# The rotary embedding of the latent keys: from the head of the query part to the place behind its projection

## The chip, the cores and the metric

The kernel runs on one core of a Trainium2 chip. The metric is the device time of one execution in microseconds (us), as the median of several runs. Engines are named as the profile names them: PE (TensorE, matrix products; PEld are its weight loads), DVE (VectorE), ACT (ScalarE), POOL (GpSimd) and SP (which only issues transfers). Each engine works through its own instructions in a fixed order, and an instruction that has to wait for another engine holds up everything behind it on its own engine.

## What is computed

One layer of a decoder with 512 positions and width 1024: a norm and an input projection, three causal token mixers side by side (RWKV-7, "FoX" forgetting attention with 4 heads of 64, and multi-head latent attention, MLA, with 4 heads), a gated merge, an output projection and a squared-ReLU MLP. The part that the change touches is the rotary embedding of the MLA keys. Cut to that:

```
q_lat, kv_lat, k_pe = split(z_c, [384, 384 + 256])        # k_pe: 64 columns, shared by all heads
q  = (rms_norm(q_lat) @ w_q_up).reshape(B, S, 4, 128 + 64)
q_pe = apply_rope(q[..., 128:], cos, sin)
k_pe = apply_rope(k_pe, cos, sin)
apply_rope(x) = concat([x1 * cos - x2 * sin, x1 * sin + x2 * cos])   # x1, x2: halves of the last axis
```

`k_pe` has 64 numbers for each of the 512 positions. The rotated keys are needed when the MLA logits are formed, the rotated queries likewise.

## The kernel before

All products are made of three matmuls each (`mm3`, lines 146 to 150): operands are split into a high and a low float32r part, and high x high, low x high and high x low are added up. ACT makes the high part and DVE the low part (`hilo`, L120 and L121), both for the weights that arrive by DMA (`wraw` to `whi` and `wlo`) and for intermediate results.

The 512 positions are 4 tiles of 128 (`NT = 4`). The order around the change is this:

1. `attn_inputs` (from L479). A product with the columns `wn` gives, for each tile of positions, 324 columns in PSUM: FoX values, the 64 columns of `k_pe` and the 4 forget gates. L521 copies the key columns to `kpe`, in four ACT instructions, one for each tile. Then `log_forget` computes the forget gates; in it POOL clears the tile `lfx` (L614), DVE copies the gates into it (L616), and PE makes their running sum from it (L627, `pcum`).
2. `attention` (from L644). A loop over heads and tiles issues logits, softmax, transposes and the product with the values, a few steps apart. Between them `fill` hands PE pieces of other projections ("fillers"): first the remaining RWKV columns, then the second pair of FoX heads (`fox_steps`), then `mla_prep`.
3. `mla_prep` (L767) is the head of the query part of MLA. It first issues the rotary embedding of the keys, for one tile of positions after the other: two products with cosine and sine (L777, L778) into a scratch tile `rope`, and a difference and a sum (L779, L780) into `kr`, all on POOL. Then, for each tile, PE makes the 256 rotary query columns in an accumulator `acc`, DVE multiplies them with cosine and sine (L777 and L778 again, with DVE as the engine), and POOL takes difference and sum into `qr`. At the end PE transposes `kr` (L799).

PE's order is written out by hand (`manual_schedule`). DVE, ACT, POOL and SP follow an order that a scheduler derives from the program; it is fixed when the kernel is built.

The scratch tile `rope` is one of the tiles `wk` (L483): 128 x 512 numbers, five buffers, used in turn also for the probabilities `p` of the softmax (L705), for `lfx`, `cum` and others. A new tile takes a buffer when the last reader of its former content is done; for a `p` this is its transposition on PE (L717, `tp<-ident,p`). The transposes have a single buffer in PSUM (`tp`): the next one waits until ACT (L721, `pth`) and DVE (L722, `ptl`) have read the one before.

Of the kernel before, what the change touches and what calls it, by code (L numbers as in the profile page):

```python
# [12 lines left out]
F32 = mybir.dt.float32  # L13
# [5 lines left out]
ALU = mybir.AluOpType  # L19
# [4 lines left out]
P = 128  # L24
S = 512
NT = S // P
# [72 lines left out]
class Builder:  # L99
# [379 lines left out]
    def attn_inputs(self, pz, zps):  # L479
        nc, a, ap = self.nc, self.a, self.ap  # L480
        self.omu = self.cp.tile([P, 16], F32, name="omu")[:, 0:8]
        nc.vector.tensor_scalar(self.omu, self.col("mu", 0, 8), -1.0, 1.0, ALU.mult, ALU.add)
        wk = lambda name: ap.tile([P, S], F32, tag="wk", name=name, bufs=5)  # L483
        self.wk = wk
        self.cstep = wk("cstep")
        nc.sync.dma_start(self.cstep, a["cstep"])
        h = self.h
        self.vt = lambda name: ap.tile([P, S], F32R, tag="v", name=name, bufs=8)
        self.fv = [self.vt(f"fv{t}") for t in range(NT)]
        wn = self.stream(a["wn"], NCG, into=[(self.vt("nh"), self.vt("nl")) for i in range(2)])  # L490
        wns = [next(wn) for i in range(WN_AHEAD)]
        lraw = [ap.tile([P, 3, S], F32, tag="pth", name="lraw", bufs=2) for _ in range(2)]
        lat = [lraw[i // 3][:, i % 3] for i in range(5)]
        for i in range(5):
            if i in LAT_DVE:
                nc.vector.tensor_copy(lat[i], zps[i])
            else:
                nc.scalar.activation(lat[i], zps[i], AF.Copy)
        self.qk = lambda name: ap.tile([P, S], F32R, tag="qk", name=name, bufs=12)
        self.fqk = [None] * 4  # L500
        self.fox_queries(0, zps[5])
        self.fox_keys(0, zps[6])
        self.kpe = ap.tile([P, NT, 64], F32, name="kpe")
        self.lf = ap.tile([P, NT, 8], F32, name="lf")[:, :, 0:4]
        pn = [pz.tile([P, NCG], F32, tag="z", name=f"n{t}") for t in range(NT)]
        self.lat = [None] * 5
        norms = [self.lat_norm(pz, lat, at, n, g) for at, n, g in ((0, 3, "qg"), (3, 2, "kvg"))]
        for kb in range(NB):
            whi, wlo = wns.pop(0)
            for t in range(NT):  # L510
                sl = slice(t * P, (t + 1) * P)
                self.mm3(pn[t], (h[0][kb][:, sl], h[1][kb][:, sl]), (whi, wlo), kb == 0, kb == NB - 1)
            wns += [w for w in (next(wn, None),) if w]
            self.some_mods(MODS_N if kb < MODS_K else 0)
            if kb in (1, 2):
                next(norms[kb - 1])
            if kb in (5, 6):
                next(norms[kb - 5])
        for t in range(NT):
            nc.vector.tensor_tensor(self.lf[:, t, :], pn[t][:, 320:324], self.col("bf", 0, 4), ALU.add)  # L520
            nc.scalar.activation(self.kpe[:, t, :], pn[t][:, 256:320], AF.Copy)  # L521
        for t in range(NT):
            fv = self.fv[t].rearrange("p (h q f) -> p h q f", h=4, q=2)
            self.hilo(fv[:, :, 0], fv[:, :, 1], pn[t][:, 0:256].rearrange("p (h f) -> p h f", h=4))
        self.log_forget()
        self.ksq = []
        self.feed = self.pieces([(a["wz"][:, (2 + i) * D:(3 + i) * D], D) for i in range(2)] + self.attn_weights())
        self.ahead = None
        self.weight()
        for i in range(2):  # L530
            ps = pz.tile([P, S], F32, tag="z", name="zz")
            for kb, _ in enumerate(self.z_steps(i, ps)):
                if (i, kb) == NORM_AT:
                    for norm in norms:
                        for _ in norm:
                            pass
                if (i, kb) == CUM_AT:
                    self.forget_cumsum(pz)

    def fox_queries(self, pair, ps):  # L540
        nc = self.nc
        for hh in range(2):
            own, oth = slice(hh * 64, hh * 64 + 64), slice(64 - hh * 64, 128 - hh * 64)
            qa, qb, ka, kb = self.fqk[2 * pair + hh] = [self.qk(n) for n in ("fqa", "fqb", "fka", "fkb")]
            nc.scalar.activation(qa[own], ps[own], AF.Copy, scale=0.125)
            nc.vector.scalar_tensor_tensor(qa[oth], ps[own], 0.125, qa[own].bitcast(F32), ALU.mult, ALU.subtract)
            nc.scalar.activation(qb[own], ps[own], AF.Copy, scale=0.125)
# [219 lines left out]
    def mla_prep(self):  # L767
        nc, a, ap, wk = self.nc, self.a, self.ap, self.wk

        def rope(src, t, nh, dst, eng):  # L770
            c = self.cos[:, t, None, None, :].broadcast_to([P, nh, 2, 32])
            s = self.sin[:, t, None, None, :].broadcast_to([P, nh, 2, 32])
            tt = wk("rope").rearrange("p (x h two f) -> p x h two f", x=2, h=4, two=2)
            t1, t2 = tt[:, 0, 0:nh], tt[:, 1, 0:nh]
            v = src.rearrange("p (h two f) -> p h two f", h=nh, two=2)
            d = dst.rearrange("p (h two f) -> p h two f", h=nh, two=2)
            eng.tensor_tensor(t1, v, c, ALU.mult)  # L777
            eng.tensor_tensor(t2, v, s, ALU.mult)  # L778
            nc.gpsimd.tensor_tensor(d[:, :, 0], t1[:, :, 0], t2[:, :, 1], ALU.subtract)  # L779
            nc.gpsimd.tensor_tensor(d[:, :, 1], t2[:, :, 0], t1[:, :, 1], ALU.add)  # L780

        self.lath = ([x[0] for x in self.lat], [x[1] for x in self.lat])
        kr = ap.tile([P, NT, 64], F32, name="kr")
        for t in range(NT):
            rope(self.kpe[:, t, :], t, 1, kr[:, t], nc.gpsimd)
        wqr = self.weight()
        self.qr = qr = ap.tile([P, NT, 256], F32, name="qr")
        for t in range(NT):
            tl = slice(t * P, (t + 1) * P)
            ps = self.acct()  # L790
            for kb in range(3):
                wl = slice(kb * 256, kb * 256 + 256)
                self.mm3(ps[:, 0:256], (self.lat[kb][0][:, tl], self.lat[kb][1][:, tl]),
                         (wqr[0][:, wl], wqr[1][:, wl]), kb == 0, kb == 2)
            rope(ps[:, 0:256], t, 4, qr[:, t], nc.vector)
            yield 1.5 * MM3
        pk = self.prw.tile([P, S], F32, tag="rw", name="pk")
        for t in range(NT):
            nc.tensor.transpose(pk[0:64, t * P:(t + 1) * P], kr[:, t], self.ident)  # L799
        self.k1 = k1 = ap.tile([P, S], F32R, name="k1")  # L800
        nc.scalar.activation(k1[0:64], pk[0:64], AF.Copy)
        nc.vector.tensor_tensor(k1[64:128], pk[0:64], k1[0:64].bitcast(F32), ALU.subtract)
# [843 lines left out]
```

## Time and profile before

| | |
|---|---|
| three runs | 876.29, 876.34, 876.96 us (median 876.34) |
| the profiled execution | 875.69 us, of which 873.9 us are the span from the first instruction to the last |
| PE busy | 845.9 us, 97% of the span |
| DVE, ACT, POOL busy | 524.8, 381.5, 95.6 us |
| mean granted PE clock | 0.989 of full speed |

A row of the timeline gives the start in us, the duration, the engine, the line, the operation, output and input tiles, shapes and the count. In brackets stands how long the engine had stood idle before the row, and what ended that. A row of a table by stage gives the stretch and its length, for each engine its busy time with the number of instructions, the granted PE clock, the share of the DMA engines and the GB/s. PE's matmuls overlap each other: the distance from start to start is the cost of one, not its duration.

### The profile page before, as it was taken

How to read it: one execution, taken by the hardware profiler on the slowest of the kernel's cores; microseconds unless marked ns; L12 is line 12 of the kernel's file. 1: busy time of each engine (PE TensorE's matmuls, PEld its weight loads, DVE VectorE, ACT ScalarE, POOL GpSimd, SP SyncE). 2: the span in 40 equal slices, each digit the busy share in tenths (PEclk: the TensorE clock that was granted, in tenths of full speed). 3: DMA queues.
4: the chain of work that ended last, by engine and by line, in shares of the span. 5: the costliest groups of instructions: out<-in, count | busy, mean ns of one | idle time of the engine just before them, and what ended most of it. 6: DMA issues, size and time to landing. Idle time of an engine off the chain costs nothing.

```text
span 873.9 us, 12074 instructions
## 1 busy us (share of the span) xinstructions
PE 845.9 (97%) x4520; PEld 699.8 (80%) x4520; DVE 524.8 (60%) x1053; ACT 381.5 (44%) x855; POOL 95.6 (11%) x129
## 2 busy tenths in 40 slices
PE   8889996999999999999999999999999999999997
PEld 6668786788877888886788889888888888888886
DVE  6998865887489755344586686442236543233465
ACT  5458663765462232424654775432314343122331
POOL 4410003000021089200000110000000000000000
PEclk9999997999999999999999999999999999999999
DMA  9764221111246732311136402432246432333311
GB/s 353 244 216 168 66 64 40 42 62 52 96 134 210 258 111 91 115 50 49 32 109 223 169 25 77 141 97 84 88 145 214 144 121 85 97 106 98 97 49 72
DMA packets 32635, 102.56 MB, mean 117 GB/s; under 512 B 5873, under 2 KB 7553, under 8 KB 31810
## 3 DMA queue, kind: packets, MB, share of 16 engines
q1 hardware_dynamic: 32002, 100.94, 34.9%
q0 software_dynamic: 288, 0.79, 0.3%
q8 instruction: 35, 0.57, 0.3%
q14 instruction: 22, 0.18, 0.1%
q10 hardware_dynamic: 288, 0.08, 0.0%
HBM read 99.16 MB, written 2.63 MB: 116 GB/s over the span
## 4 chain that ended last, share of the span: by engine, by line
PE 84%; DVE 9%; ACT 3%; issue 2%; DMA 1%; POOL 1%; SPq 0%; DVEq 0%; POOLq 0%; ACTq 0%
PE acc L148 24%; PE acc L150 23%; PE acc L149 23%; DVE wm L219 2%; DVE wlo L463 1%; PE z L472 1%; PE tp L717 1%; DMA xt<-xT 1%; DVE hl L464 1%; DVE mod L428 1%; PE pu L1027 1%; PE pr L1186 1%; DMA wm<-wmod 0%; PE py L1203 0%; PE pv L734 0%
## 5 line engine op out<-in xcount | busy, mean ns | idle before, releaser
L121 DVE TENSOR_TENSOR wlo<-wraw,whi 128x512 fp32r<-128x512 f32 (+4 forms) x260 | 165.6, 656 | 197.5 <-ACT whi L120 197.1
L120 ACT ACTIVATE whi<-wraw 128x512 fp32r<-128x512 f32 (+4 forms) x260 | 145.3, 587 | 295.1 <-PE acc L149 178.1
L148 PE MATMUL acc<-g,whi 128*128 128x512 f32 (+1 forms) x304 | 108.3, 356 | 0.0
L149 PE MATMUL acc<-g,whi 128*128 128x512 f32 (+1 forms) x304 | 108.1, 356 | 0.0
L150 PE MATMUL acc<-g,wlo 128*128 128x512 f32 (+1 forms) x304 | 108.1, 356 | 0.0
L148 PE MATMUL acc<-hh,whi 128*128 128x512 f32 x256 | 105.2, 411 | 0.0
L150 PE MATMUL acc<-hh,wlo 128*128 128x512 f32 x256 | 100.4, 392 | 0.6 <-DVE wlo L121 0.6
L149 PE MATMUL acc<-wlo,uh 128*128 128x512 f32 (+1 forms) x262 | 100.8, 385 | 0.0
L148 PE MATMUL acc<-whi,uh 128*128 128x512 f32 (+1 forms) x262 | 100.7, 384 | 0.0
L150 PE MATMUL acc<-whi,ul 128*128 128x512 f32 (+1 forms) x262 | 100.7, 384 | 0.0
L149 PE MATMUL acc<-hl,whi 128*128 128x512 f32 x256 | 100.1, 391 | 0.0
L219 DVE SCALAR_TENSOR_TENSOR wm<-wm,crow 128x1024 f32<-128x1024 f32 x41 | 52.2, 1274 | 24.1 <-DMA wm<-wmod 24.1
L148 PEld LDWEIGHTS acc<-g,whi 128*128 128x128 f32 x304 | 57.5, 189 | 8.2
L150 PEld LDWEIGHTS acc<-g,wlo 128*128 128x128 f32 x304 | 57.5, 189 | 8.1
L149 PEld LDWEIGHTS acc<-g,whi 128*128 128x128 f32 x304 | 57.5, 189 | 8.1
L150 PEld LDWEIGHTS acc<-hh,wlo 128*128 128x128 f32 x256 | 48.1, 188 | 11.7 <-DVE wlo L121 1.0
L149 PEld LDWEIGHTS acc<-wlo,uh 128*128 128x128 f32 x262 | 49.2, 188 | 10.1 <-DVE wlo L121 0.4
L150 PEld LDWEIGHTS acc<-whi,ul 128*128 128x128 f32 x262 | 49.2, 188 | 9.8
L148 PEld LDWEIGHTS acc<-whi,uh 128*128 128x128 f32 x262 | 49.2, 188 | 9.8
L148 PEld LDWEIGHTS acc<-hh,whi 128*128 128x128 f32 x256 | 48.5, 190 | 10.1 <-issue 0.2
L149 PEld LDWEIGHTS acc<-hl,whi 128*128 128x128 f32 x256 | 48.3, 189 | 8.1
L706 ACT ACTIVATE p<-sc,nb 128x128 f32<-128x128 f32 (+3 forms) x32 | 16.8, 526 | 28.3 <-DVE nb L704 14.7
(435 smaller groups left out, 1485.9 us busy)
## 6 DMA issues: line engine op xcount, KB each, us to landing
wm<-wmod SPq DMA_DIRECT2D x36, 512.0 KB, 4.3
wraw<-wu SPq DMA_DIRECT2D x32, 512.0 KB, 3.3
wraw<-wd SPq DMA_DIRECT2D x24, 512.0 KB, 3.3
wraw<-wgb SPq DMA_DIRECT2D x16, 512.0 KB, 3.4
wm<-wmod SPq DMA_DIRECT2D x6, 1024.0 KB, 6.8
wraw<-wz SPq DMA_DIRECT2D x10, 512.0 KB, 3.4
wraw<-wga SPq DMA_DIRECT2D x8, 512.0 KB, 3.6
wraw<-wo SPq DMA_DIRECT2D x8, 512.0 KB, 4.4
```

Of the source, the lines that this page charges most:

```text
L120: nc.scalar.activation(hi, src, AF.Copy)
L121: nc.vector.tensor_tensor(lo, src, hi.bitcast(F32), ALU.subtract)
L148: mm(out, lhs[0], rhs[0], start=start, stop=False)
L149: mm(out, lhs[0], rhs[1], start=False, stop=False)
L150: mm(out, lhs[1], rhs[0], start=False, stop=stop)
L219: self.nc.vector.scalar_tensor_tensor(w, w, 0.5, self.crow[:, cols], ALU.mult, ALU.mult, accum_out=dst)
L428: nc.vector.scalar_tensor_tensor(A, acc[0], b1[:, d:d + 1], self.col("gpre", d), ALU.add, ALU.mult)
L463: nc.vector.tensor_tensor(wlo, raw, whi.bitcast(F32), ALU.subtract)
L464: nc.vector.scalar_tensor_tensor(lo, t, B, hi.bitcast(F32), ALU.add, ALU.subtract)
L472: nc.tensor.matmul(zps[i], w[:, i * P:(i + 1) * P], r, start=first and w is whi and r is hi, stop=last and r is lo)
L706: nc.scalar.activation(p[:, 0:n], ps[:, 0:n], AF.Exp, bias=nb, scale=scale, accum_out=den)
L717: nc.tensor.transpose(tp[:, kb, :], p[:, kb * P:(kb + 1) * P], self.ident)
```

## The change

The key part leaves `mla_prep` and becomes a method of its own, `key_rope`. It is called in `attn_inputs` right behind the four copies into `kpe`. It does all four tiles of positions at once: four POOL instructions (two products over 4 x 64 numbers for each partition, a difference and a sum over 4 x 32), where there were sixteen. It takes one scratch tile `rope`, where the old code took four. The local function `rope` in `mla_prep` is left with the queries alone, and always multiplies on DVE.

```
             nc.scalar.activation(self.kpe[:, t, :], pn[t][:, 256:320], AF.Copy)
+        self.key_rope()
         for t in range(NT):
...
+    def key_rope(self):
+        pool, shp = self.nc.gpsimd, [P, NT, 2, 32]
+        self.kr = self.ap.tile([P, NT, 64], F32, name="kr")
+        tt = self.wk("rope").rearrange("p (x t two f) -> p x t two f", x=2, t=NT, two=2)
+        v, d = (x.rearrange("p t (two f) -> p t two f", two=2) for x in (self.kpe, self.kr))
+        pool.tensor_tensor(tt[:, 0], v, self.cos[:, :, None, :].broadcast_to(shp), ALU.mult)
+        pool.tensor_tensor(tt[:, 1], v, self.sin[:, :, None, :].broadcast_to(shp), ALU.mult)
+        pool.tensor_tensor(d[:, :, 0], tt[:, 0, :, 0], tt[:, 1, :, 1], ALU.subtract)
+        pool.tensor_tensor(d[:, :, 1], tt[:, 1, :, 0], tt[:, 0, :, 1], ALU.add)
...
-            eng.tensor_tensor(t1, v, c, ALU.mult)
-            eng.tensor_tensor(t2, v, s, ALU.mult)
+            nc.vector.tensor_tensor(t1, v, c, ALU.mult)
+            nc.vector.tensor_tensor(t2, v, s, ALU.mult)
...
-        kr = ap.tile([P, NT, 64], F32, name="kr")
-        for t in range(NT):
-            rope(self.kpe[:, t, :], t, 1, kr[:, t], nc.gpsimd)
+        kr = self.kr
...
-            rope(ps[:, 0:256], t, 4, qr[:, t], nc.vector)
+            rope(ps[:, 0:256], t, 4, qr[:, t])
```

On PE, DVE, ACT and SP every instruction keeps its place. Only POOL's order changes. The first excerpt is POOL before, from the last product of the conditioning (`wm`) to the first tile of positions of the key part; three more groups like it follow, and then the query part (`qr`).

```order
L222 TENSOR_TENSOR wm<-wm,crow 128x1024
L614 MEMSET lfx 128x512
L777 TENSOR_TENSOR rope<-kpe,cos 128x64
L778 TENSOR_TENSOR rope<-kpe,sin 128x64
L779 TENSOR_TENSOR kr<-rope 128x32
L780 TENSOR_TENSOR kr<-rope 128x32
```

The second is POOL of the changed kernel at the same place (its lines are shifted: L546 to L549 are `key_rope`, L625 clears `lfx`).

```order
L222 TENSOR_TENSOR wm<-wm,crow 128x1024
L546 TENSOR_TENSOR rope<-kpe,cos 128x256
L547 TENSOR_TENSOR rope<-kpe,sin 128x256
L625 MEMSET lfx 128x512
L548 TENSOR_TENSOR kr<-rope 128x4x32
L549 TENSOR_TENSOR kr<-rope 128x4x32
L790 TENSOR_TENSOR qr<-rope 128x4x32
L791 TENSOR_TENSOR qr<-rope 128x4x32
```

The key part now runs as soon as `kpe` is there, and its two products stand ahead of the clearing of `lfx`.

The third excerpt is DVE of the changed kernel, where `mla_prep` begins: `fkb` belongs to the last FoX head, `rope` is the first tile of the rotary queries, `ptl` the low part of transposed probabilities, `nb` a softmax maximum. These rows stand in the same order before, under the lines 121, 561, 777, 555, 778, 722 and 702.

```order
L121 TENSOR_TENSOR wlo<-wraw,whi 128x512
L572 TENSOR_SCALAR fkb<-cum,cols 64x512
L788 TENSOR_TENSOR rope<-acc,cos 128x256
L566 TENSOR_TENSOR fkb<-acc,fka 64x512
L789 TENSOR_TENSOR rope<-acc,sin 128x256
L733 TENSOR_TENSOR ptl<-tp,pth 128x2x128
L713 TENSOR_REDUCE nb<-sc 128x1
```

Nothing moved here. What differs is what the first `rope` row waits for. Before, its scratch buffer is the one that the last tile of the key part used, so it waits for POOL's last `kr` row and for PE. In the changed kernel the buffer is free of POOL's work: it waits for PE alone, for the two transposes that read the old content.

More of the change, by code (lines that the diff above doesn't have):

```diff
@@ L768, in mla_prep, with rope @@
         nc, a, ap, wk = self.nc, self.a, self.ap, self.wk
-        def rope(src, t, nh, dst, eng):
+        def rope(src, t, nh, dst):
             c = self.cos[:, t, None, None, :].broadcast_to([P, nh, 2, 32])
```

## The prediction

> **What bounds the kernel now.** I read the page first, then PE's waits, then the stretch in which PE stands still, engine by engine.
>
> ```profile
> PE   845.9 (97%) x4520; PEld 699.8 (80%) x4520; DVE 524.8 (60%) x1053; ACT 381.5 (44%) x855; POOL 95.6 (11%) x129
> ...
> PEclk9999997999999999999999999999999999999999
> ```
>
> PE is the bound: 97% of the span. What can be won is either work of PE, which the change leaves alone, or one of its few gaps. One slice of the clock line is not 9: the seventh, from 131 to 153 us, the stretch of the key part. PE's waits by cause, and then its timeline there:
>
> ```profile
> PE z L472 <- ACT hh L462: 7.7, 5, 3.0
> PE tp L717 <- DVE ptl L722: 7.1, 2, 6.9
> ```
> ```profile
> 128.49 0.28 PE L148 MATMUL acc<-whi,lath 128*128 128x256 f32 x1
> ...
> 129.57 0.38 PE L717 MATMUL tp<-ident,p 128*128 128x128 f32 x2
> ...
> 131.31 0.28 PE L150 MATMUL acc<-whi,latl 128*128 128x256 f32 x1
> 138.50 0.87 PE L717 MATMUL tp<-ident,p 128*128 128x128 f32 x3 [6.91 <-DVE ptl L722]
> ...
> 139.71 0.52 PE L148 MATMUL acc<-whi,lath 128*128 128x256 f32 x1
> ...
> 143.65 0.81 PE L717 MATMUL tp<-ident,p 128*128 128x128 f32 x4
> 144.22 0.36 PE L759 MATMUL sc<-fka,fqa 128*128 128x256 f32 x1
> ```
>
> The longest gap of the kernel is here: PE stands still from 131.59 to 138.50, 6.91 us, because the transposes want the one `tp` buffer, which DVE's `ptl` row has not read yet. Who holds up DVE:
>
> ```profile
> 132.09 0.53 DVE L561 TENSOR_SCALAR fkb<-cum,cols 64x512 fp32r<-64x512 f32 x1
> 136.41 0.42 DVE L777 TENSOR_TENSOR rope<-acc,cos 128x256 f32<-128x256 f32 x1 [3.79 <-POOL kr L780]
> 136.87 0.69 DVE L555 TENSOR_TENSOR fkb<-acc,fka 64x512 fp32r<-64x512 f32 x1
> 137.60 0.42 DVE L778 TENSOR_TENSOR rope<-acc,sin 128x256 f32<-128x256 f32 x1
> 137.94 0.41 DVE L722 TENSOR_TENSOR ptl<-tp,pth 128x256 fp32r<-128x256 f32 x1
> ...
> 141.14 0.48 DVE L708 TENSOR_SCALAR p<-p,rden 128x512 f32<-128x512 f32 x1
> ```
> ```profile
> 130.08 0.62 POOL L777 TENSOR_TENSOR rope<-kpe,cos 128x64 f32<-128x64 f32 x1 [55.11 <-PE tp L717]
> ...
> 135.25 0.32 POOL L777 TENSOR_TENSOR rope<-kpe,cos 128x64 f32<-128x64 f32 x1
> ...
> 136.13 0.25 POOL L780 TENSOR_TENSOR kr<-rope 128x32 f32<-128x32 f32 x1
> ```
>
> DVE's rotary query row waits 3.79 us for POOL's last key row, and `ptl` stands three rows behind it. POOL had been idle for 55 us: it could not start because its scratch buffer was held by probabilities until the transposes at 129.57. So the chain is PE's transposes, sixteen POOL rows (130.08 to 136.38), DVE's `rope`, `fkb`, `rope`, `ptl`, PE. The part of the 6.91 us that POOL causes is DVE's 3.79; the other 3.1 is DVE's own queue.
>
> The second cost of the gap is the clock. By stage, with two stretches of the start-up for comparison:
>
> ```profile
> 24.63:28.04 3.41, 0.45 (x3) 0.07 (x1) 3.38 (x4) 0.84 (x2) 1.67 (x1) 1.00 0.83 295
> 28.04:31.45 3.41, 3.41 (x8) 2.71 (x9) 3.34 (x7) 2.46 (x5) 1.05 (x1) 0.50 0.64 178
> 130.43:133.84 3.41, 1.16 (x10) 0.95 (x9) 2.17 (x5) 1.72 (x4) 3.18 (x8) 1.00 0.20 28
> 133.84:137.25 3.41, 0.00 (x0) 0.00 (x0) 0.80 (x2) 0.00 (x0) 2.23 (x9) 0.50 0.17 68
> 137.25:140.67 3.42, 2.17 (x11) 2.20 (x12) 2.49 (x7) 1.76 (x4) 1.70 (x4) 0.50 0.00 0
> 140.67:144.08 3.41, 3.41 (x18) 3.41 (x18) 1.97 (x7) 0.65 (x3) 0.91 (x3) 0.50 0.02 5
> 144.08:147.50 3.42, 3.42 (x23) 3.08 (x23) 2.93 (x8) 2.29 (x6) 0.88 (x2) 1.00 0.00 0
> ```
>
> The granted clock (the column behind POOL's) is 1.00 or 0.50 over whole stretches of 3.41 us, and all its changes lie on one grid of that step: down at 28.04, up at 31.45, down at 133.84, up at 144.08 (133.84 is 31 steps behind 28.04). A stretch in which PE works 0.45 or 1.16 us is followed by half clock. One with 3.41 us of work is followed by full clock, one with 2.17 us (at half clock) is not. So after the gap PE runs at half clock from 138.50 to 144.08.
>
> **The change part by part.**
>
> *The sixteen POOL rows go from the gap.* DVE's `rope` row then waits for PE alone, for transposes that started at 129.57, and for its accumulator, done by then. DVE reaches the row when the `fkb` row ends, 132.09 + 0.53 = 132.62, instead of 136.41. Nothing between it and `ptl` waits for anything new (the high part of `fkb`, which ACT makes, comes nearest; its row is the first below), so `ptl` and PE's restart move from 138.50 to about 134.73. **Term 1: 3.77 us.** A gap of 131.59 to 134.73, 3.1 us, stays: next late is DVE's queue itself, in which these rows then follow each other without a pause.
>
> ```profile
> 132.22 0.59 ACT L554 ACTIVATE fka<-acc 64x512 fp32r<-64x512 f32 x1
> ```
>
> *The clock behind the gap.* At half clock the work from 138.50 to 144.22 took 5.72 us. Nine matmuls of 256 columns take 1.08 us at full clock (128.49 to 129.57), and eighteen 3.94 at half (139.71 to 143.65), so 9 take 1.97: full clock needs 0.55 of the time. The gap thus cost another 0.45 x 5.72 = 2.6 us. What is left of this cost behind a gap of 3.1 us is not shown by any row at this place; the bounds:
>
> - nothing left, if the clock stays up: 0 us. The next transposes (143.65) then need DVE's row `p` (L708, 141.14 to 141.62), which ends at least 3.77 us earlier, by 137.9; PE would be there at 134.73 + 0.55 x 5.15 = 137.56. that costs 0.3 us at most.
> - one step of the grid at half clock: 0.45 x 3.41 = 1.5 us.
> - two steps: 0.45 x 6.83 = 3.1 us.
>
> The rows nearest in size are these, PE's gaps at start-up:
>
> ```profile
> 27.97 3.33 PE L472 MATMUL z<-hh,whi 128*128 128x512 f32 x7 [2.96 <-ACT hh L462]
> ...
> 46.79 1.88 PE L472 MATMUL z<-hh,whi 128*128 128x512 f32 x7 [2.15 <-ACT hh L462]
> ```
>
> The gap of 2.96 us was followed by exactly one step at half clock (28.04 to 31.45), the one of 2.15 us by none:
>
> ```profile
> 45.11:48.52 3.41, 1.73 (x8) 1.43 (x9) 3.34 (x7) 2.51 (x4) 0.00 (x0) 1.00 0.77 267
> ```
>
> A stretch with 1.73 us of work keeps the clock, one with 1.16 loses it; I put the limit between, at 1.4, or 2.0 us of idleness. A gap of 3.14 us leaves every stretch with less idleness than that only when the grid cuts it between 1.14 and 2.0 us from its start: for 0.86 of 3.41 us, one position in four. At the position of this execution it is lost at 133.84 as before. I take one step, 1.5 us. **Term 2: 2.6 - 1.5 = 1.1 us won.**
>
> [...]
>
> *The four new POOL rows.* They start when the last copy into `kpe` ends, at about 86.4.
>
> ```profile
> 16.10 2.35 POOL L222 TENSOR_TENSOR wm<-wm,crow 128x1024 f32<-128x1024 f32 x1 [4.79 <-DMA wm<-wmod]
> ...
> 74.45 0.53 POOL L614 MEMSET lfx<- 128x512 f32 x1 [22.27 <-DVE ssum L580]
> ...
> 138.10 0.45 POOL L779 TENSOR_TENSOR qr<-rope 128x128 f32<-128x128 f32 x1 [1.72 <-DVE rope L778]
> ```
> ```profile
> 86.00 0.44 ACT L521 ACTIVATE kpe<-n 128x64 f32<-128x64 f32 x2
> ```
> ```profile
> 91.90 0.30 DVE L616 COPY lfx<-lf 128x64 f32<-128x64 f32 x2
> ```
> ```profile
> 96.46 2.32 PE L627 MATMUL pcum<-cstep,lfx 128*128 128x512 f32 x8
> ```
>
> The sum and the difference (128 numbers) cost 0.45 each. The products have 256 numbers: between 0.45 (128) and 2.35 (1024), nearest to the first; I take 0.75. Behind them `lfx` is cleared, at 74.45 before, now from 86.4 + 1.5 to about 88.5, at worst 86.4 + 4.7 + 0.53 = 91.7. DVE wants it at 91.90. So this costs nothing: DVE's wait for the forget gates hides it. If that cover went, the next is 4.4 us wide, from 92.1 to PE's `pcum` at 96.46. `kr` itself is read by PE only at the end of `mla_prep`.
>
> *The rest.* POOL's queue behind the old place holds only the query rows, which wait for DVE and come earlier with it. The weights that PE needs behind the gap are there in time:
>
> ```profile
> 132.20 0.33 SPq L133 DMA_DIRECT2D wraw<-wqk  x1
> ```
> ```profile
> wraw<-wqk SPq DMA_DIRECT2D x1, 320.0 KB, 2.9
> ```
> ```profile
> 143.89 0.83 ACT L120 ACTIVATE whi<-wraw 128x320 fp32r<-128x320 f32 x2 [1.58 <-PE acc L150]
> ```
>
> Issued at 132.20, landed at about 135.1, split at 143.89, which moves to about 139: still 4 us to spare. Later loads are issued as buffers come free behind PE, so they move along.
>
> **Sum.** 3.77 + 1.1 = 4.9 us. The profiled execution took 875.69 us and would take 870.8; it was 0.65 us quicker than the median of the runs, 876.34. From the median: **871.5 us**.
>
> **The rivals.**
>
> 1. *The clock stays up.* For it: a gap of 2.15 us kept it, and the new gap can be cut by the grid. Against it: 2.96 us did not. Gain 3.77 + 2.6 = 6.4: 870.0 us.
> 2. *Half clock for two steps.* For it: at the position of this execution the clock falls at 133.84, and the stretch up to 137.25 would hold 2.5 us of work; one of 2.17 did not bring the clock back. Gain 3.77 + 2.6 - 3.1 = 3.3: 873.0 us.
> 3. *The gain is hidden or doesn't come*: the query row waits for something else that the profile now puts down to POOL, such as the transposes that freed the buffer. Against it: they started at 129.57, 2.5 us before DVE is there. Or DVE and ACT, which PE waits for again in the later softmax steps, don't move with PE. Their inputs come from PE, so they should. 876 us.
> 4. *Slower*: the two products stand ahead of `lfx` and block it, and DVE, in whose queue the copies at 91.90 stand ahead of the weights' low parts, waits. POOL's rows get longer beside DVE: the first `rope` row took 0.62 us, and the last, with DVE idle, 0.32. To turn 4.9 us of gain into a loss of 1.8, the clearing has to end 6.7 us later than the cover of 4.4 us behind 91.9 allows: at 103, with products of some 8 us each. The price would be the excess over 96.3 us, 878.1 us at that point.
>
> **How the numbers follow.** Forecast (one step at half clock) 0.55; clock stays up 0.20; two steps 0.14; hidden 0.09; slower 0.02. The range takes in the first three, 0.89 in all: from 870.0 less the 0.2 us of a cut of the gap that I may have read too long, 869.8, to 873.0 with the 0.6 us by which the runs of before lie above their median, 873.6. Two tenths of a per cent, 1.75 us, is about what a measurement of this kernel can tell from no change: faster 0.55 + 0.20 + 0.14 = 0.89, same 0.09, slower 0.02.
>
> **What would show it.** DVE's first rotary query row starts at about 132.7 with no wait for POOL; PE's gap before the three transposes is about 3.1 us instead of 6.9; the key rows on POOL lie between 86 and 91 us, and no wait for `lfx` stands on DVE. The clock is at half for one step of 3.41 us (or none, or two) behind the gap, on a grid of that step. All that PE does from 150 us on comes earlier by the same amount. The prediction is wrong if the gap stays near 6.9 us, if another wait in DVE's queue takes its place, or if PE's start at 150 us is earlier by 5 us and its end is not.

## The result, and the profile after

The changed kernel took 871.32 us (median of 4 runs, 870.06 to 871.96), the kernel before 876.32 us (median of 4, 874.73 to 876.96): a ratio of 0.9944, with a 95% interval from 0.9925 to 0.9962. A second measurement, beside the experiments, gave 871.39 us and 0.9943 (0.9930 to 0.9956). The profiled execution took 870.71 us, with a span of 868.9 us where it was 873.9.

The page of the changed kernel, the same rows as before:

```profile
PE 845.6 (97%) x4520; PEld 699.3 (80%) x4520; DVE 526.2 (61%) x1053; ACT 381.3 (44%) x855; POOL 93.8 (11%) x117
...
PEclk9899999999999999999999999999999999999999
```

PE's busy time is the same only in sum. Between PE's restart behind the gap and the last row of its timeline below, it fell by 1.14 us (5.72 to 4.58); elsewhere it is 0.8 us longer in this execution, 0.43 of that ahead of 128.4 us. With the idleness that went, the span is 5.0 us shorter. The 7 in the seventh slice of the clock line is gone (the 8 in the second slice is start-up: half clock from 26.75 to 33.58 us in this execution, from 28.04 to 31.45 in the one before). PE's waits by cause:

```profile
PE z L472 <- ACT hh L462: 7.0, 5, 3.0
PE tp L728 <- DVE ptl L733: 3.2, 2, 3.0
```

The longest wait fell from 6.9 to 3.0 us. Now DVE's timeline of the changed kernel (start, duration, line), around the first rotary query row:

```profile
131.95 0.53 DVE L572 TENSOR_SCALAR fkb<-cum,cols 64x512 fp32r<-64x512 f32 x1
132.41 0.41 DVE L788 TENSOR_TENSOR rope<-acc,cos 128x256 f32<-128x256 f32 x1
...
133.92 0.41 DVE L733 TENSOR_TENSOR ptl<-tp,pth 128x256 fp32r<-128x256 f32 x1
```

The query row follows without a wait. PE's timeline there:

```profile
131.18 0.29 PE L150 MATMUL acc<-whi,latl 128*128 128x256 f32 x1
134.47 0.52 PE L728 MATMUL tp<-ident,p 128*128 128x128 f32 x3 [3.01 <-DVE ptl L733]
...
138.34 1.05 PE L728 MATMUL tp<-ident,p 128*128 128x128 f32 x4
139.05 0.52 PE L770 MATMUL sc<-fka,fqa 128*128 128x256 f32 x1
```

The gap is 3.01 us instead of 6.91: 3.90 us won. From the restart to the last row shown it takes 4.58 us instead of 5.72: 1.14 won. By stage, cut on the 3.41 us grid of this execution:

```profile
132.58:135.99 3.41, 1.52 (x13) 1.55 (x14) 3.04 (x7) 1.64 (x5) 0.98 (x3) 1.00 0.35 96
135.99:139.40 3.41, 3.41 (x18) 3.41 (x17) 1.94 (x7) 1.48 (x6) 1.65 (x4) 0.50 0.02 5
139.40:142.81 3.41, 3.41 (x23) 3.02 (x23) 3.31 (x10) 1.77 (x5) 0.88 (x2) 1.00 0.00 0
```

One step at half clock is left (0.50 in the second row), where there were three. POOL has the key part here:

```profile
86.44 0.75 POOL L546 TENSOR_TENSOR rope<-kpe,cos 128x256 f32<-128x256 f32 x1 [35.16 <-ACT kpe L521]
87.14 0.74 POOL L547 TENSOR_TENSOR rope<-kpe,sin 128x256 f32<-128x256 f32 x1
87.81 0.54 POOL L625 MEMSET lfx<- 128x512 f32 x1
```

The clearing of `lfx` ends at 88.35, long before DVE's copies.

### The profile page after: what moved, and what is told of

Same layout as the page of the kernel before. It is cut to its first block, busy times and chain, and to the rows that moved or that the text cites. A ratio compares the mean times of both kernels' runs of the same rounds, so it can differ in the third digit from the quotient of the medians.

```text
span 868.9 us, 12056 instructions
## 1 busy us (share of the span) xinstructions
PE 845.6 (97%) x4520; PEld 699.3 (80%) x4520; DVE 526.2 (61%) x1053; ACT 381.3 (44%) x855; POOL 93.8 (11%) x117
## 4 chain that ended last, share of the span: by engine, by line
PE 83%; DVE 10%; ACT 3%; DMA 2%; issue 2%; SPq 0%; DVEq 0%; ACTq 0%
PE acc L148 23%; PE acc L150 23%; PE acc L149 23%; DVE mod L428 1%; DVE wm L219 1%; PE z L472 1%; DVE wlo L121 1%; PE tp L728 1%; DMA xt<-xT 1%; DVE wlo L463 1%; DMA wraw<-wo 1%; DVE hl L464 1%; PE pu L1036 1%; PE pr L1195 1%; ACT whi L120 0%
## 5 line engine op out<-in xcount | busy, mean ns | idle before, releaser
L219 DVE SCALAR_TENSOR_TENSOR wm<-wm,crow 128x1024 f32<-128x1024 f32 x41 | 50.1, 1221 | 26.3 <-DMA wm<-wmod 26.1
```

The lines of the kernel that those rows point to most:

```text
L219: self.nc.vector.scalar_tensor_tensor(w, w, 0.5, self.crow[:, cols], ALU.mult, ALU.mult, accum_out=dst)
```

## The experiments

The theory: POOL's sixteen rows could not start before the transposes because their scratch was a rotating buffer; they held up DVE for 3.8 us, DVE held up PE, and the gap cost again through the clock. The rivals: the place in the program or the batching does it; the clock costs nothing; POOL's work at its new place costs something.

**Where the wait came from: three half-changes.** First the changed kernel again, as a yardstick:

> The changed kernel once more, beside the kernels that it is compared with. Theory (DVE's wait for POOL is gone, and what is left of the clock's loss depends on where the 3.41 us grid cuts the gap of 3.0 us): 870.0 to 872.0 us, 4 to 6 us below the kernel before, with runs that differ among themselves by one half-clock step of about 1.5 us. Rival (a fixed loss behind the gap): runs within 0.3 us of each other.

It took 871.39 us, with runs from 870.26 to 872.62. The scatter, 2.4 us, is more than one half-clock step (1.5 us by the prediction). The kernel before scatters as well (875.02 to 878.26 in 11 runs), so this alone does not show where the scatter is from.

Then the wide instructions at the old place:

```
-        self.key_rope()                 # in attn_inputs
...
+        self.key_rope()                 # at the head of mla_prep
         kr = self.kr
```

> The four wide POOL instructions, but issued at the old place, at the head of the query part, with the scratch tile that waits for the transposes. Theory A (the length of POOL's block behind the transposes makes the wait): POOL starts at about 130.1 us and needs 2.5 us by the rows of the changed kernel (0.75, 0.74, 0.45, 0.45), up to 3.5 beside DVE; DVE's first query row waits 0 to 1 us instead of 3.8; time 871.3 to 872.5 us. Theory B (it has to be moved ahead, the block costs its wait wherever it is short or long): DVE waits 3 us or more, 875 to 876 us.

872.70 us, ratio 0.9961 (0.9946 to 0.9976). POOL, DVE and the stages of this run:

```profile
129.62 1.03 POOL L545 TENSOR_TENSOR rope<-kpe,cos 128x256 f32<-128x256 f32 x1 [55.13 <-PE tp L727]
...
132.35 0.63 POOL L548 TENSOR_TENSOR kr<-rope 128x128 f32<-128x128 f32 x1
```
```profile
133.01 0.42 DVE L787 TENSOR_TENSOR rope<-acc,cos 128x256 f32<-128x256 f32 x1 [0.35 <-POOL kr L548]
```
```profile
133.90:137.31 3.41, 2.21 (x11) 2.25 (x12) 2.48 (x8) 1.75 (x4) 1.74 (x4) 0.50 0.17 67
137.31:140.72 3.41, 3.41 (x18) 3.41 (x18) 1.93 (x7) 0.69 (x3) 0.88 (x3) 0.51 0.02 5
140.72:144.10 3.38, 3.38 (x23) 3.04 (x22) 2.96 (x8) 2.25 (x6) 0.87 (x2) 1.00 0.00 0
```

Theory A: DVE waits 0.35 us, not 3.8, although POOL starts as late as ever. Most of the gain needs no move at all, only a shorter block. The time is 0.2 us above the forecast range: POOL's and DVE's rows meet here (the first product took 1.03 us instead of 0.75, and DVE's `p` row beside it 0.78 us instead of 0.42), PE's gap was 3.96 us, and two steps ran at half clock.

Next the kernel before with its sixteen rows at their old place, and only the scratch changed (`qr`, in which it now lies, is allocated ahead of the key part for that):

```
-            tt = wk("rope").rearrange("p (x h two f) -> p x h two f", x=2, h=4, two=2)
+            tt = qr[:, NT - 1, 0:128] if nh == 1 else wk("rope")
+            tt = tt.rearrange("p (x h two f) -> p x h two f", x=2, h=nh, two=2)
```

> The kernel before with its sixteen narrow POOL instructions at their old place in the program; only the scratch of the key part is not taken from the rotating buffers, but lies in the part of qr that is written last. Theory A (POOL's late start is the wait for the scratch buffer and nothing else): POOL does the key part at about 86 to 93 us, right behind the clearing of lfx, DVE's first query row waits for nothing at about 132.6 us, and the time is that of the changed kernel, 871.3 us plus or minus 0.7. Theory B (the place in the program decides): POOL starts at about 130 us as before, 876.3 us.

870.62 us, ratio 0.9939 (0.9925 to 0.9953). POOL of this run:

```profile
85.11 0.44 POOL L778 TENSOR_TENSOR qr<-kpe,cos 128x64 f32<-128x64 f32 x1 [10.30 <-ACT kpe L521]
...
90.73 0.26 POOL L781 TENSOR_TENSOR kr<-qr 128x32 f32<-128x32 f32 x1
```

This settles the cause. POOL's order in the program is that of before, and yet the key part runs 45 us earlier, as soon as its input is there. The rotating buffer alone had kept it back. PE's gap in this run was 3.04 us.

And the move without the batching (sixteen narrow rows in `key_rope`, a loop over `t` with the old four instructions):

> The new place with the sixteen narrow instructions and the rotating scratch tiles. Theory A (the move alone is enough): POOL works from 86.4 to about 93 us, the clearing of lfx among its rows and later than in the changed kernel, DVE's copies into lfx wait up to 1 us, PE does not; 871.3 us plus or minus 0.7. Theory B (the batching carries a part of the gain): above 872.5 us.

870.62 us, ratio 0.9936 (0.9923 to 0.9949). POOL worked from 86.14 to 91.95 us; the gap was 3.01 us. Theory A: the batching adds nothing that can be measured once the work is out of the gap. DVE's wait for `lfx`, which I allowed up to 1 us, did not come. (The profiled execution was the slowest of the six, 872.56 us, with two steps at half clock behind the gap.)

**What the clock costs.** Here nothing is taken away: matmuls that write to a PSUM tile which is overwritten later fill the gap.

```
+            if t == 1:               # behind the second tile of query products
+                pk = self.prw.tile([P, S], F32, tag="rw", name="pk")
+                for _ in range(26):  # 12 in the changed kernel
+                    nc.tensor.matmul(pk, self.identr, self.h[0][0], start=True, stop=True)
             yield 1.5 * MM3
-        pk = self.prw.tile([P, S], F32, tag="rw", name="pk")
```

> The kernel before, with 26 matmuls of 512 columns (0.23 us each, 6.0 us) put on PE at the start of its gap of 6.9 us, behind the second tile of the query products; they write into the PSUM tile pk, whose content is overwritten later. DVE's wait for POOL stays as it is. Theory (the gap costs 2.6 us a second time through the half clock behind it): the clock stays at 1.00, PE restarts at 138.5 us as before, the next four transposes come at about 141.3 us instead of 143.65, and the time falls by 2.3 to 2.6 us to 873.7. Rival (DVE sets the pace behind the gap, the clock costs nothing): 876.3 us, PE waits again before the four transposes.

873.09 us, ratio 0.9966 (0.9953 to 0.9979). PE's timeline of this run, and its clock behind the gap:

```profile
132.06 6.13 PE L799 MATMUL pk<-hh,identr 128*128 128x512 f32 x26
139.13 0.52 PE L717 MATMUL tp<-ident,p 128*128 128x128 f32 x3 [0.95 <-DVE ptl L722]
141.96 0.60 PE L717 MATMUL tp<-ident,p 128*128 128x128 f32 x4
```
```profile
138.00:144.00 6.00, 5.05 (x42) 4.76 (x41) 4.80 (x15) 3.79 (x10) 2.79 (x6) 1.00 0.01 3
```

DVE waits for POOL as before (3.8 us), and PE restarts no earlier: 7.20 us behind the start of the last query product ahead of it (131.93), where it was 7.19 (from 131.31); the rows are 0.6 us later here (POOL's first `rope` at 130.70, 130.08 before). Still 2.5 us are won (875.57 to 873.09): from restart to the next four transposes it takes 2.83 us instead of 5.15. The 2.6 us that the prediction puts down to the clock behind the old gap are real, and of that size.

> The changed kernel with 12 such matmuls (2.8 us) in its gap of 3.0 us. Theory (one half-clock step of 1.5 us is left in most executions): the clock stays at 1.00 behind the gap, the time falls by 1.0 to 1.6 us against the changed kernel, to about 870.0, and the runs lie closer together. Rival (nothing is left of the clock's loss, or DVE sets the pace): 871.3 us.

869.24 us, ratio 0.9924 (0.9912 to 0.9937), runs from 868.43 to 869.59: 2.1 us below the changed kernel, more than the 1.0 to 1.6 expected. All five runs lie below all nine of the changed kernel (870.06 to 872.62), though the intervals of the two ratios overlap a little. The clock stayed at 1.00. PE of this run:

```profile
131.40 2.96 PE L808 MATMUL pk<-hh,identr 128*128 128x512 f32 x12
134.58 0.52 PE L728 MATMUL tp<-ident,p 128*128 128x128 f32 x3 [0.22 <-DVE ptl L733]
...
137.49 0.63 PE L728 MATMUL tp<-ident,p 128*128 128x128 f32 x4
```

2.91 us from restart to the four transposes, against 3.87 in the changed kernel. Together with the transposes themselves (0.38 us to the next row, 0.71 there) that is 1.3 us for one step at half clock, and the two profiled executions differ by just this much (870.71 and 869.41 us). The executions with two steps, in the run with sixteen rows moved and the one batched in place, took 5.15 us from restart to the four transposes. Where the rest of the 2.1 us between the medians is from, no trace shows.

**What is left of the gap.** DVE's products for a tile of queries issued one step later:

```
-            rope(ps[:, 0:256], t, 4, qr[:, t])
             yield 1.5 * MM3
+            rope(ps[:, 0:256], t, 4, qr[:, t])
```

> The changed kernel, with DVE's products for a tile of rotary queries issued one step later in the program, so that the low part of the transposed probabilities stands ahead of the first query row on DVE. Theory (the 3.0 us that are left of the gap are DVE's own queue): PE restarts at about 133.0 us instead of 134.5, the gap shrinks to 1.5 us, the clock stays up; but the fourth tile of query products needs the accumulator that the first one gives back later, and waits about 1.2 us. Sum 1.3 us won against the changed kernel, 870.0 us; 868.3 if that wait does not come. Rival (ACT's high parts or the p buffers set the restart): gap 3.0 us as now, 871.3 us or more.

870.27 us, ratio 0.9932 (0.9919 to 0.9946). PE of this run:

```profile
133.40 0.55 PE L728 MATMUL tp<-ident,p 128*128 128x128 f32 x3 [1.41 <-DVE ptl L733]
...
135.15 0.48 PE L148 MATMUL acc<-whi,lath 128*128 128x256 f32 x1 [0.92 <-ACT fka L567]
```

The gap fell to 1.41 us as forecast, and a wait of 0.92 us came behind it. But its cause was not the one I named (the accumulator of the first query tile, which DVE gives back): it was ACT's copy of the last FoX keys, which the scheduler had put behind the transposes' high part. And the clock fell all the same: the matmuls from 135.42 to 138.63 came 0.21 us apart instead of 0.12. The two waits seem to have done this together: the matmuls come closer again at about 138.7, so by an estimate from PE's rows the step ahead of the fall was 131.9 to 135.3, which takes in both waits and held 1.09 us of PE work, less than the 1.52 with which the clock fell in the changed kernel. The gain over the changed kernel, 1.1 us, is within what the two intervals allow as nothing.

With five matmuls in the gap beside it:

> The late query rows together with matmuls in what they left of the gap: five of 512 columns (1.15 us) behind the second tile of query products. Theory (gap and clock are separate terms and add up): the clock stays at 1.00 although PE still waits about 0.9 us for ACT's copy of the last FoX keys, and the time falls below both of its parts (the late rows alone 870.27, the filled gap alone 869.24), by about 0.4 us against the filled gap: 868.8. Rival (ACT and DVE set the pace of that step, so what the restart gains is lost a few rows later): 869.2 us or more.

868.88 us, ratio 0.9925 (0.9912 to 0.9937). The wait for ACT was there as before (0.91 us) and the first one nearly gone (0.26 us); the clock stayed at 1.00, so the wait for ACT alone did not bring it down here. The order of the medians is that of the theory, but the 0.4 us between this and the filled gap alone is less than either run's scatter, and the ratios to the kernel before, 0.9925 and 0.9924, don't tell them apart. Whether gap and clock add up here stays open.

The four rows of FoX heads 2 and 3 on POOL:

```
-            self.nc.vector.tensor_scalar(dst[oth], self.cum[oth].bitcast(F32), self.col("cmul", k)[oth],
+            eng = self.nc.vector if hd < 2 else self.nc.gpsimd
+            eng.tensor_scalar(dst[oth], self.cum[oth].bitcast(F32), self.col("cmul", k)[oth],
```

> The changed kernel with the four rows that put the running sum into the operands of FoX heads 2 and 3 (fqb and fkb, 0.55 us each on DVE, two of them in the stretch ahead of the gap) on POOL, which is idle there. Theory A (what is left of the gap is the length of DVE's queue): PE restarts about 1.1 us earlier, the gap falls from 3.0 to about 1.9 us, the clock stays up in most executions, 869.0 to 870.0 us. Theory B (POOL's rows slow the DVE rows beside them, as in the run with the longer POOL work, and give part of it back): gap 2.3 to 3.0 us, 870.3 to 871.4 us.

868.65 us, ratio 0.9925 (0.9912 to 0.9939): the lowest median of all, without any idle work, and by the ratio level with the two runs that fill the gap. All five runs (867.59 to 870.01) lie below the nine of the changed kernel. PE and POOL of this run:

```profile
133.93 0.52 PE L729 MATMUL tp<-ident,p 128*128 128x128 f32 x3 [1.98 <-DVE ptl L734]
```
```profile
103.24 1.93 POOL L573 TENSOR_SCALAR fqb<-cum,cols 64x512 fp32r<-64x512 f32 x2 [13.40 <-DVE cum L644]
117.80 1.64 POOL L573 TENSOR_SCALAR fkb<-cum,cols 64x512 fp32r<-64x512 f32 x2 [12.63 <-DVE p L720]
```

The gap is 1.98 us, shorter by the two rows that left DVE's queue (theory A), and the clock did not fall. POOL needed 0.8 to 1.0 us for a row for which DVE needed 0.55, far from where anybody waits.

**What POOL's work costs at its new place.**

```
-        pool.tensor_tensor(tt[:, 1], v, self.sin[:, :, None, :].broadcast_to(shp), ALU.mult)
+        for _ in range(9):
+            pool.tensor_tensor(tt[:, 1], v, self.sin[:, :, None, :].broadcast_to(shp), ALU.mult)
```

> The changed kernel with POOL's product with the sine done nine times instead of once, 6 us more ahead of the clearing of lfx. Theory (PE's running sum has a cover of some 4 us behind DVE's copies): the clearing ends at about 94.5 us instead of 88.4, DVE waits 1.5 to 2.5 us for it ahead of its copies, PE waits for nothing new, and the time stays within 0.5 us of the changed kernel. Rival (DVE's queue is tight there, the wait goes through to PE): 873 to 874 us.

872.97 us, ratio 0.9970 (0.9959 to 0.9980), above the changed kernel by 1.6 us and so the rival's time, but not on its way. The run did not test what it was made for: the scheduler put the clearing of `lfx` behind the first of the nine products, so it ended at 88.7. POOL, DVE and PE of this run:

```profile
88.67 6.88 POOL L548 TENSOR_TENSOR rope<-kpe,sin 128x256 f32<-128x256 f32 x8
```
```profile
89.95 0.70 DVE L617 TENSOR_SCALAR fu<-fe 128x16 f32<-128x16 f32 x1
```
```profile
107.23 0.33 PE L772 MATMUL sc<-fkb,fqb 128*128 128x128 f32 x1 [1.25 <-DVE fkb L573]
```

It showed something else. Beside POOL's products DVE's rows were longer: the rows from `fe` to the copies into `lfx` took 2.3 us more in sum than in the changed kernel (6.2 against 3.9), and the rows behind them came that much later. PE's running sum, which reads the copies, does not wait even so, but PE's first FoX logits wait 1.25 us for DVE's `fkb`. What POOL adds there is not paid through `lfx`, but through DVE. The 1.25 us are most of the 1.6; the rest is not assigned.

## Why the prediction was right, point by point

- **The bound, and the chain of the wait**: right. The run with its own scratch shows the buffer as the cause, the one with the wide rows in place shows the length of the block as the rest.
- **Term 1, 3.77 us**: 3.90 by the gap. The gap that was left, 3.01 us against 3.1 forecast, is DVE's queue, as the run with two rows fewer in it confirms.
- **Term 2, 1.1 us** (2.6 less one step of 1.5): 1.14 in the profiled execution, with one step at half clock. That there is one step was a choice, not a rule, and that this one execution hit the term to 0.04 us is luck: of the five profiles with a gap of 3.0 us at this place (changed kernel twice, own scratch, sixteen rows moved, longer POOL work) four had one step and one had two, and the wide rows in place, with a gap of 3.96 us, had two. The kernel before with a filled gap won 2.5 of the 2.6 us.
- **The limit at 1.4 us of work in a step**: too low. The step from 132.58 held 1.52 us of work and the clock fell. In the profiles before and after, from 20 us on, every step with 1.52 us or less was followed by half clock, and none with 1.73 us or more was; at half clock the clock stayed down behind steps with up to 2.75 us of work and came back behind those worked through, 3.41 us (last section). With the two limits anywhere between these, and the grid anywhere, a gap of 3.0 us would cost no step at 0.11 to 0.23 of the positions, two at 0.13 to 0.39 and one at 0.44 to 0.70. This is an estimate from those steps; the chances of 0.20, 0.55 and 0.14 lie within it.
- **The first rival, the clock stays up**, did not come in any of the seven profiles with a gap of 3.0 us or more at this place, though the filled gaps show that its price was about right (1.3 to 2.1 us below the forecast case; 1.5 forecast). In the changed kernel a step that PE idled for 55% (132.58 to 135.99, 1.52 us of work in 3.41) was followed by half clock.
- **The third rival, the gain is hidden**, did not come: PE's row at 144.22 us before starts at 139.05, 5.17 us earlier, and the span ends 5.0 us earlier, so behind the gap nearly nothing was lost again.
- **The new POOL rows at 0.75 us, the clearing done by 88.5**: 0.75 and 0.74, and 88.35.
- **"This costs nothing, the next cover is 4.4 us wide"**: nothing was lost, but the cover that I named was not the nearest. DVE's rows beside POOL became longer, and its copies into `lfx` moved from 91.90 to 92.75 us while the rows ahead had come 0.1 us earlier. Two rows, before and after:

```profile
88.71 0.17 DVE L605 TENSOR_SCALAR fu<-fe 128x16 f32<-128x16 f32 x1
...
103.08 1.13 DVE L561 TENSOR_SCALAR fkb<-cum,cols 64x512 fp32r<-64x512 f32 x2
```
```profile
89.30 0.43 DVE L616 TENSOR_SCALAR fu<-fe 128x16 f32<-128x16 f32 x1
...
103.93 1.13 DVE L572 TENSOR_SCALAR fkb<-cum,cols 64x512 fp32r<-64x512 f32 x2
```

  The first `fkb` ends about 0.57 us after its start (half of 1.13), at 103.65 before and 104.50 after. PE's logits that read it started at 105.50 before, without a wait:

```profile
105.50 0.28 PE L760 MATMUL sc<-fkb,fqb 128*128 128x128 f32 x1
```

  So the cover there was about 1.9 us, and the change used up 0.9 of it. The slower rival was priced by the wrong way through: 6.9 us of further POOL work, not two products of 8 us, were enough to lose 1.6 us of the gain.
- **The sum**: 4.9 us forecast; 5.0 by the medians and by the spans.

## What to carry to other kernels

When an engine with little to do starts late, ask which buffer it waits for before moving its code: a scratch tile from a rotating pool ties a side task to work with which it has nothing in common. The gap of the matrix engine was paid twice here: 6.91 us as the gap, and 2.5 us through the half-clock steps behind it, as the filled gap shows. Behind the gaps of 3.0 us and more at this place the clock fell; behind the one of 1.98 us it did not, though behind two of 1.41 and 0.92 us, 0.8 us apart, it did. So shortening a gap can be worth more than the time that it is shortened by. And work given to an idle engine can slow its neighbour (here a DVE row took 0.43 us instead of 0.17): look for the nearest reader behind that neighbour, not for the reader of the moved result.

## What the runs showed of the hardware that was not expected

- The granted clock went by the work within steps of 3.41 us. In the profiles before and after, all its changes lie on one grid of that step; in the five other profiles with a gap of 3.0 us or more that was not filled it was at half for 3.4 or 6.8 us behind the gap. From 20 us on, a step with 1.52 us of PE work (after, 132.58 to 135.99) took it to half, one with 1.73 (before, 45.11 to 48.52) kept it. At half clock, steps with 2.17 us (before), 2.44 us (after, 26.75 to 30.16) and 2.21 us (wide rows in place) did not bring it back, and one with 2.85 us of the run with sixteen rows moved didn't either (these rows are cut 0.1 us behind the grid; on it, the step holds 2.75 us):

```profile
134.89:138.30 3.41, 2.85 (x14) 2.88 (x15) 2.52 (x8) 1.41 (x4) 1.74 (x4) 0.50 0.11 44
138.30:141.70 3.40, 3.40 (x18) 3.40 (x18) 1.30 (x6) 1.30 (x5) 0.88 (x2) 0.51 0.02 5
```

  Every step worked through (3.41 us) brought it back. So a step that PE restarted in could be too short of work to bring the clock back, and one gap cost two steps at half clock in this run and in the one with the wide rows in place. Ahead of 20 us it went otherwise: before, the step from 10.96 to 14.38 held 3.13 us of PE work, 2.1 us of it matmuls of a single column (`sums`, 128x1), and was followed by half clock (14.38 to 17.79).
- DVE's and POOL's rows were longer beside each other. The same DVE row on 128 x 16 numbers took 0.17 us with POOL idle, 0.43 beside the key part and 0.70 beside the longer POOL work, whose eight products took 0.86 us each instead of 0.74. Not every row was hit: the row behind that one, of the same kind and size, took 0.17 us beside the longer POOL work too. Why the one row and not the other, no trace here shows.
